# A two-layer hybrid transformer block: the odd layer's entry reordered and its second output projection begun inside the last attention block

## The chip, the cores and the metric

The kernel runs on one core of a Trainium2 chip. The metric is the device time of one execution in microseconds; a version's time is the median of its runs. The profile is that of a single execution, taken by the hardware profiler. The engines are TensorE (PE, with its weight loads as PEld), VectorE (DVE), ScalarE (ACT), GpSimd (POOL) and SyncE (SP), which issues most of the DMAs.

## What is computed

The reference runs two layers on 512 rows of x and, in the first, on 256 rows of context (ctx), all of width 1024, in float32. Layer 0 mixes with a gated MLP and a differential attention, layer 1 with a sliding-window attention with sinks. Each layer ends with a gated FFN. The change lies in layer 1's mixer and in the seam before it:

```python
a = modulate(h, norm1_g[l], sh1, sc1)            # rmsnorm(h)*(1+scale)+shift
ac = modulate(hc, norm1_g[l], csh1, csc1)
q, k, v = split(a @ w_qkv)                       # 16 heads of 64 for q, 4 for k and v
q, k = rope(q), rope(k)
kc, vc = split(ac @ w_qkv[:, 1024:])             # ctx gives keys and values only
# per block of 128 queries: scores on a band of 384 keys and on the 256 of ctx, and a sink
p = softmax([q @ k_band + mask, q @ kc, sink])
y = (p @ [v_band, vc]) @ w_out
h = h + g1 * y
h = h + g2 * swiglu(modulate(h, norm2_g[l], sh2, sc2))
```

## The kernel before, in words

Activations lie transposed: eight tiles of 128 features by 512 rows for x and by 256 for ctx. Every float32 operand of a large product is split into a rounded high part and the rest, and a product is three matmuls (`mm3`, L110, lines L114 to L116): high by high, high by rest, rest by high. A weight piece of 128 x 512 thus needs a DMA (SP), a cast (ScalarE) and a subtraction (POOL or VectorE); `unit` (L80) does this with a ring of raw buffers and slots, and `blocks` (L94) and `dense` (L104) build a full product from it. The class attribute `dve_lo` (L71) sends every n-th subtraction of `unit` to VectorE; at 0 all go to POOL.

PSUM has eight banks: four in a fixed pool (three `bank`, L52, and one `fill`, L55), and four in a second pool that is used as two `wide` of two banks each (L58) or as four `single` (L61), and is released and opened again where its use changes.

The order of instructions on each engine comes from two sources. The framework's scheduler orders them by program order as priority and by when operands and buffers come free in its own timeline. Where `run` (L46) is used, the order is written out by hand: each instruction is issued after the engine's previous one of this chain (`tail`). `issue_after` sets such an order for single instructions. The seam is chained by hand, the odd attention is not.

The seam (`seam`, L1312) goes from layer 0's FFN to layer 1's attention. It ends the FFN's last products, squares the new rows (`square`, L1346), sums them over the features by matmuls with a matrix of ones (`sums`, L1354), turns the sum of each row into a reciprocal root on the diagonal of a tile by ten small VectorE instructions (`diagonal`, L1362) and spreads it over the partitions by one more matmul (`spread`, L1381). That is the rstd of the norm. `mod` (L1427) then makes the modulated tiles: VectorE, ScalarE, and a rest on VectorE that is called later ("l"). A list of steps (L1471) interleaves for k = 0 to 7 the modulation of x ("t", "l"), the residuals of ctx ("c") and the weight loads ("w"); `products` (L1458) issues the products of x along a second list (L1455): "K" and "V" are keys and values of tile k, "s" the sums of ctx, "d" its spread. POOL adds six of ctx's squares to tile 0 after "l4", so that "s" sums two tiles. After V7 come the first of eight query projections (q0, into `fill`), ctx's keys and values for k = 0 to 7 (L1499), the rope of the keys, the stack of high and rest parts of the keys (`stack`, L1513), and copies of mask, identity and sink on VectorE (L1529).

The odd attention (`odd`, L1547) has four groups g of four heads and four query blocks i, done as two halves of two blocks. `project_q` (L1555) projects two heads, applies the rope (`rope`, L259: VectorE and POOL) and stacks (`stack_q`, L267: ScalarE and VectorE, L272 to L278). `softmax` (L1565) computes for each of four heads x the scores into a `wide` (L1584, mask L1589, ctx L1592), the maximum (L1595, L1596), the exponential (L1598) and the sums. `attend` (L1609) transposes the result through `bank` tiles (L1621), copies it (L1624), multiplies with V (L1632), and scales by the reciprocal sums, transposed at L1643, on VectorE (L1645). `keep` (L1649) splits the result for the output projection. In the first half the projections of the queries stand between the groups; the second half runs with the output projection of the first half as filler.

`project` (L1666) does the output projection of one half for m = 0 to 7 with `dense`, adds to the residual (L785) and sums squares (L798, L802). Between its two calls stand the rstd of the first half (`ffn_rstd`, L850, into `fill`), the splits of the second half, the opening of the FFN's pool (`ffn_open`, L813), and `ffn_mod` (L853), which modulates the first half of the FFN's input. The FFN (`ffn`, L869) starts with `direct` products (L973) and ends with the final norm.

## Time and profile before

| | us |
|---|---|
| median of 3 runs | 1585.23 (1578.97 to 1585.93) |
| profiled execution | 1583.56 |
| its span, first to last instruction | 1581.5 |
| mean granted TensorE clock | 0.988 |

The profiled execution is 1.67 us below the median. Three stages matter for the change:

| stage, us from the span's start | what runs |
|---|---|
| 920 to 990 | seam: ctx's rstd, K and V, first queries |
| 990 to 1184 | odd attention |
| 1184 to 1250 | second output projection, start of the FFN |

The profile's lines read "start, length, engine, line, operation, out<-in, shape"; a bracket gives the engine's idle time before the instruction and what ended it. A line L49 stands for everything that goes through `run`, so there the tile's name tells the step: `sq` for squares and sums, `sm` for the small tiles of a diagonal, `q` or `t` for a diagonal tile or a modulated one, `pw` for a tile of the second PSUM pool, `pb` for a bank, `pf` for the fill bank. In a table of stages each row has the stage, its length, the busy time and the count of instructions of PE, PEld, DVE, ACT and POOL, the granted clock as a share of full speed, the DMA share and GB/s.

### The profile page before, as it was taken

How to read it: one execution, taken by the hardware profiler on the slowest of the kernel's cores; microseconds unless marked ns; L12 is line 12 of the kernel's file. 1: busy time of each engine (PE TensorE's matmuls, PEld its weight loads, DVE VectorE, ACT ScalarE, POOL GpSimd, SP SyncE). 2: the span in 40 equal slices, each digit the busy share in tenths (PEclk: the TensorE clock that was granted, in tenths of full speed). 3: DMA queues.
4: the chain of work that ended last, by engine and by line, in shares of the span. 5: the costliest groups of instructions: out<-in, count | busy, mean ns of one | idle time of the engine just before them, and what ended most of it. 6: DMA issues, size and time to landing. Idle time of an engine off the chain costs nothing.

```text
span 1581.5 us, 24959 instructions
## 1 busy us (share of the span) xinstructions
PE 1520.5 (96%) x9547; PEld 1355.7 (86%) x9547; DVE 1082.6 (68%) x1942; ACT 728.7 (46%) x1486; POOL 831.6 (53%) x562
## 2 busy tenths in 40 slices
PE   6999988999999999999999998999999999999998
PEld 4776877889989999999999987777869989999997
DVE  4720788765697787888786478665667976666665
ACT  2412676553553333333333345555655644444444
POOL 0463211060356776777776454531304399898982
PEclk9999999999999999999999999999999999999999
DMA  9845100033123333444552211100225233333301
GB/s 329 309 143 190 40 8 1 1 133 134 67 75 119 114 110 118 140 160 141 166 167 67 74 58 42 61 28 4 72 81 198 68 96 106 97 107 105 100 21 54
DMA packets 53415, 162.26 MB, mean 103 GB/s; under 512 B 6192, under 2 KB 8624, under 8 KB 45616
## 3 DMA queue, kind: packets, MB, share of 16 engines
q1 hardware_dynamic: 46240, 135.37, 25.6%
q10 hardware_dynamic: 7056, 25.30, 4.9%
q8 instruction: 75, 1.23, 0.3%
q14 instruction: 44, 0.36, 0.1%
HBM read 158.55 MB, written 2.10 MB: 102 GB/s over the span
## 4 chain that ended last, share of the span: by engine, by line
PE 85%; DVE 10%; ACT 3%; issue 1%; POOL 0%; DMA 0%; DVEq 0%; SPq 0%; ACTq 0%; POOLq 0%
PE pw L114 11%; PE pw L115 11%; PE pw L116 11%; PE pb L115 9%; PE pb L114 8%; PE pb L116 8%; PE pf L114 4%; PE pf L115 4%; PE pf L116 4%; PE pb L1632 2%; PE pb L1621 2%; PE pf L370 2%; PE pw L1584 1%; PE pw L1592 1%; PE pw L553 1%
## 5 line engine op out<-in xcount | busy, mean ns | idle before, releaser
L114 PE MATMUL pw<-ax,w 128*128 128x384 f32 (+2 forms) x732 | 233.9, 321 | 2.5 <-DVE q L49 1.9
L115 PE MATMUL pw<-ax,w 128*128 128x384 f32 (+2 forms) x732 | 233.8, 320 | 1.4 <-DVE ax L477 1.4
L116 PE MATMUL pw<-ax,w 128*128 128x384 f32 (+2 forms) x732 | 233.2, 319 | 0.1
L785 DVE SCALAR_TENSOR_TENSOR xT<-pb,mod,xT 128x512 f32<-128x512 f32 (+3 forms) x206 | 144.1, 706 | 128.8 <-PE pb L116 128.5
L91 POOL TENSOR_TENSOR w<-raw,w 128x512 fp32r<-128x512 f32 (+1 forms) x74 | 112.8, 1531 | 204.3 <-ACT w L88 182.0
L49 POOL TENSOR_TENSOR w<-raw,w 128x512 fp32r<-128x512 f32 x120 | 182.4, 1537 | 47.1 <-ACT w L49 47.0
L49 POOL TENSOR_TENSOR w<-t,w 128x512 fp32r<-128x512 f32 x99 | 148.1, 1499 | 56.0 <-ACT w L49 56.0
L114 PE MATMUL pb<-hh,w 128*128 128x512 f32 x480 | 171.4, 357 | 2.3 <-DVE xT L785 2.3
L116 PE MATMUL pb<-hh,w 128*128 128x512 f32 x480 | 171.8, 358 | 0.3 <-DVE w L49 0.3
L115 PE MATMUL pb<-hh,w 128*128 128x512 f32 x480 | 171.5, 357 | 0.0
L115 PE MATMUL pw<-T,w 128*128 128x384 f32 (+1 forms) x508 | 157.0, 310 | 1.2 <-DVE T L131 1.2
L114 PE MATMUL pw<-T,w 128*128 128x384 f32 (+1 forms) x508 | 156.3, 310 | 1.1 <-DVE hs L49 1.1
L116 PE MATMUL pw<-T,w 128*128 128x384 f32 (+1 forms) x508 | 157.0, 310 | 0.0
L114 PEld LDWEIGHTS pw<-ax,w 128*128 128x128 f32 x732 | 139.0, 190 | 9.5 <-DVE q L49 2.6
L115 PEld LDWEIGHTS pw<-ax,w 128*128 128x128 f32 x732 | 139.3, 190 | 7.7 <-DVE ax L477 3.1
L116 PEld LDWEIGHTS pw<-ax,w 128*128 128x128 f32 x732 | 139.5, 191 | 3.0 <-DVE w L954 0.4
L114 PE MATMUL pf<-ax,w 128*128 128x256 f32 (+2 forms) x412 | 136.9, 332 | 3.9 <-ACT f L596 2.8
L115 PE MATMUL pf<-ax,w 128*128 128x256 f32 (+2 forms) x412 | 136.1, 330 | 0.8 <-POOL ax L131 0.8
L116 PE MATMUL pf<-ax,w 128*128 128x256 f32 (+2 forms) x412 | 135.6, 329 | 0.0
L49 POOL TENSOR_TENSOR hh<-hs,hh 128x768 fp32r<-128x768 f32 (+1 forms) x42 | 80.8, 1925 | 90.0 <-ACT hh L49 67.6
L49 POOL TENSOR_TENSOR w<-rawo,w 128x512 fp32r<-128x512 f32 x59 | 104.1, 1764 | 29.8 <-ACT w L49 29.8
L239 DVE SCALAR_TENSOR_TENSOR junk<-ar,cb 128x1024 bf16<-128x1024 f32 x64 | 105.7, 1652 | 0.0
(403 smaller groups left out, 3961.4 us busy)
## 6 DMA issues: line engine op xcount, KB each, us to landing
raw<-ffn_in SPq DMA_DIRECT2D x44, 1024.0 KB, 5.2
ar<-ada SPq DMA_DIRECT2D x24, 1024.0 KB, 7.2
ar<-ada ACTq DMA_DIRECT2D x48, 512.0 KB, 3.5
rawo<-ffn_out SPq DMA_DIRECT2D x88, 256.0 KB, 3.0
raw<-odd_out SPq DMA_DIRECT2D x32, 256.0 KB, 2.7
raw<-qk SPq DMA_DIRECT2D x16, 256.0 KB, 7.6
raw<-uv SPq DMA_DIRECT2D x16, 256.0 KB, 2.7
raw<-even_out SPq DMA_DIRECT2D x8, 512.0 KB, 3.5
```

Source lines behind the costliest of these rows:

```text
L49: self.tail[key] = fn(*args, **kw)
L91: eng.tensor_tensor(lo, raw, hi.bitcast(F32), ALU.subtract)
L114: mm(out, s[0], m[0], start=start, stop=False, **kw)
L115: mm(out, s[0], m[1], start=False, stop=False, **kw)
L116: return mm(out, s[1], m[0], start=False, stop=stop, **kw)
L239: return self.nc.vector.scalar_tensor_tensor(junk, t, 1.0, self.cb[who], ALU.mult, ALU.mult, accum_out=self.acc[who][:, col:col + 1])
L370: nc.tensor.matmul(ps[32 * q:32 * q + 32, :w], cst[:, k, :], t[:, w * q:w * q + w], start=k == 0, stop=k == KT - 1, skip_group_check=True)
L553: nc.tensor.matmul(ps[:, :TX], Q[c][:, qs], K[c][p][:, :TX], start=p == 0, stop=p == 1)
L785: ins = self.nc.vector.scalar_tensor_tensor(h, ps[:, r], self.modcol(l, j, m, who), h, ALU.mult, ALU.add)
L1584: nc.tensor.matmul(ps[:, st:en], Q, K[g][p][:, b0 * P:b1 * P], start=p == 0, stop=p == 1, skip_group_check=True)
L1621: last = nc.tensor.transpose(pt[:, x * P:(x + 1) * P], es[2 * (x % 2) + x // 2][:, kb * P:(kb + 1) * P], self.ident)
L1632: nc.tensor.matmul(po[64 * h:64 * h + 64, :], V[vb][:, 64 * g:64 * g + 64], t[:, h * TC:h * TC + TC], start=kb == 0, stop=kb == nb - 1, sk ...
```

## The change

In the seam, the sums of ctx move in front of K5 and take six squares directly ("s" over tiles 0, 3 to 7); only tiles 1 and 2 are added to tile 0 beforehand, one by VectorE and one by POOL. The squares of x get fewer buffers. The weights of two query projections (q0, q1) are loaded, and both projections follow V7, ahead of ctx's keys and values; q1 goes into a `single`. Mask, identity, sink and its exponential are made by ScalarE earlier, and the rope of the keys is issued before the query projections. In `odd`, the rope and stack of q0 and q1 are issued at the priority of the point after the first keys' stack, before the second PSUM pool is opened as `wide`; their stacks lie in another pool. At the end, all of the first six splits of the second half are made by VectorE, outputs m = 0 and 1 of the second projection begin with k = 0 to 5 in the fill bank, ordered after the second and the third score of the last block (g 3, i 3) and one after the other, with four weight slots taken in an order by halves of k. The spread of the first half's rstd moves behind that and into a `wide`, `ffn_mod` comes after the seventh split, and `project` finishes m = 0 and 1 with k = 6 and 7 before it goes on with m = 2.

```diff
...
-    def stack_q(self, q, pool, T, tag, bufs, s=1.0, eng=None):
+    def stack_q(self, q, pool, T, tag, bufs, s=1.0, eng=None, out=None):
         nc = self.nc
-        qa = pool.tile([P, T], F32R, name=self.uid("qa"), tag=tag, bufs=bufs)
-        qb = pool.tile([P, T], F32R, name=self.uid("qb"), tag=tag, bufs=bufs)
+        qa, qb = out or [pool.tile([P, T], F32R, name=self.uid(v), tag=tag, bufs=bufs) for v in ("qa", "qb")]
         A, B = slice(0, 64), slice(64, 128)
...
             T = (TX, TC)[who]
-            sq[who, m] = Qp.tile([P, T], F32, name=self.uid("sq"), tag=f"sq{who}", bufs=8)
+            tag, n = ("sqc", 8) if who else ("sqx", 3) if m in (0, 3, 7) else ("sqt", 2)
+            sq[who, m] = Qp.tile([P, T], F32, name=self.uid("sq"), tag=tag, bufs=n)
             run("ACT", nc.scalar.activation, sq[who, m], self.h(who, m), AF.Square)
...
             c_residual(m)
+        add("DVE", 1, 0, 1)
         c_unit(2, self.bank)
...
-        order = iter("K0 V0 K1 V1 K2 V2 K3 V3 K4 V4 K5 V5 K6 s K7 V6 d V7".split())
+        order = iter("K0 V0 K1 V1 K2 V2 K3 V3 K4 V4 s K5 V5 K6 V6 K7 d V7".split())
         csum = []
...
                     csum.append(self.single())
-                    sums(csum[0], [sq[1, 0], sq[1, 7]], TC)
+                    sums(csum[0], [sq[1, m] for m in (0, 3, 4, 5, 6, 7)], TC)
                 elif v == "d":
...
-        rests = {}
+        rests, Wq = {}, []
         for v in "t0 c5 l0 w t1 c6 t2 l1 w c3 t3 l2 w c4 t4 l3 w c7 t5 l4 t6 l5 t7 l6 l7".split():
...
                 rests.pop(k)()
-                products(f"V{k}" if k < 5 else "V5" if k == 5 else "s" if k == 6 else "K7")
-            if v == "l4":
-                for m in range(1, 7):
-                    add("POOL", 1, 0, m)
-            elif v == "l5":
+                products(f"V{k}" if k < 7 else "K7")
+            if v == "l1":
+                add("POOL", 1, 0, 2)
+            elif v in ("l5", "l7"):
                 wide, (self.ring, self.ring_cfg) = (self.ring, self.ring_cfg), kept
-                Wq = [part(*load(a["q1"][0][:, c:c + 512])) for c in (0, 512)]
+                Wq.append([part(*load(a["q1"][len(Wq)][:, c:c + 512])) for c in (0, 512)])
                 self.ring, self.ring_cfg = wide
...
         products("V7")
-        qps = self.fill()
-        for k in range(KT):
-            t, c = Wq[k // 4], k % 4 * P
-            run("PE", self.mm3, qps, (t[:, 0, c:c + P], t[:, 1, c:c + P]), X[k], k == 0, k == KT - 1)
+        mask = Rk.tile([P, 2, P], F32R, name="mask")
+        identr = Rk.tile([P, P], F32R, name="identr")
+        sink = Rk.tile([P, 16], F32, name="sink2")
+        run("ACT", nc.scalar.copy, mask, mraw.rearrange("p (a c) -> p a c", a=3)[:, 0::2, :])
+        run("ACT", nc.scalar.copy, identr, self.ident)
+        run("ACT", nc.scalar.copy, sink, nsink)
+        run("ACT", nc.scalar.mul, nsink, nsink, -1.0)
+        run("ACT", nc.scalar.activation, self.small(16), nsink, AF.Exp)
+        kfs = [Rt.tile([P, TA], F32, name=self.uid("kf"), tag="kf", bufs=2) for _ in range(2)]
+        for n in range(2):
+            self.rope(kps[n], kfs[n][:, :TX], tabs)
+        qps = [self.fill(), self.single()]
+        for ps, W2 in zip(qps, Wq):
+            for k in range(KT):
+                t, c = W2[k // 4], k % 4 * P
+                run("PE", self.mm3, ps, (t[:, 0, c:c + P], t[:, 1, c:c + P]), X[k], k == 0, k == KT - 1)
         kc = self.single()
...
                 v_c(k - 1)
-        kfs = [Rt.tile([P, TA], F32, name=self.uid("kf"), tag="kf", bufs=2) for _ in range(2)]
         K = []
-        for n in range(2):
-            self.rope(kps[n], kfs[n][:, :TX], tabs)
         for n in range(2):
...
             stack(n, slice(0, TX))
-        for n in range(2):
             nc.scalar.copy(kfs[n][:, TX:], kc[n])
             stack(n, slice(TX, TA))
-        mask = Rk.tile([P, 2, P], F32R, name="mask")
-        identr = Rk.tile([P, P], F32R, name="identr")
-        sink = Rk.tile([P, 16], F32, name="sink2")
-        with tc.issue_after(self.tail["DVE"].ins):
-            nc.vector.tensor_copy(mask, mraw.rearrange("p (a c) -> p a c", a=3)[:, 0::2, :])
-            nc.vector.tensor_copy(identr, self.ident)
-            nc.vector.tensor_copy(sink, nsink)
-            nc.vector.tensor_scalar(nsink, nsink, -1.0, None, ALU.mult)
-        with tc.issue_after(self.tail["ACT"].ins):
-            nc.scalar.activation(self.small(16), nsink, AF.Exp)
+            if n == 0:
+                here = tc.cur_priority
         V = []
...
         Rt.release()
+        self.here = here
         self.kv = qps, X, Rk, tabs, K[0] + K[1], V, mask, identr, sink, nsink
...
         tc, nc, a = self.tc, self.nc, self.a
-        self.wp.release()
-        self.open_wide()
         qps, X, Rk, tabs, K, V, mask, identr, sink, nsink = self.kv
         Rs = tc.alloc_tile_pool(name="att1", bufs=1, side="right", reuse_waits="tile")
-        Qs = {}
+        Qs, scored = {}, {}
+        stacks = [Rk.tile([P, TX], F32R, name=self.uid(t), tag="sq01", bufs=4) for _ in range(2) for t in ("qa", "qb")]
         def project_q(n):
-            ps = (self.bank if n == 1 else self.fill)() if n else qps
-            if n:
+            ps = self.fill() if n > 1 else qps[n]
+            if n > 1:
                 with tc.issue_after(self.tail["ACT"].ins) if n < 3 else ExitStack():
...
                 self.dense(ps, W, X)
-            qf = Rs.tile([P, TX], F32, name=self.uid("qf"), tag="qf", bufs=2)
+            qf = Rs.tile([P, TX], F32, name=self.uid("qf"), tag="qf", bufs=2) if n > 1 else self.tmp()
             self.rope(ps, qf, tabs)
-            Qs[n] = self.stack_q(qf, Rs, TX, "sq", 16, 0.125)
+            Qs[n] = self.stack_q(qf, Rs, TX, "sq", 12, 0.125, out=stacks[2 * n:2 * n + 2])
...
                 for p in range(2):
-                    nc.tensor.matmul(ps[:, en:en + TC], Q, K[g][p][:, TX:], start=p == 0 and not edge, stop=p == 1,
-                                     skip_group_check=True)
+                    last = nc.tensor.matmul(ps[:, en:en + TC], Q, K[g][p][:, TX:], start=p == 0 and not edge,
+                                            stop=p == 1, skip_group_check=True)
+                scored[g, i, x] = last
                 c = nm[:, x:x + 1]
...
-        raw = {}
+        raw, self.kept = {}, {}
...
             t = t[:, :TC], t[:, TC:TX]
-            self.split(*t, raw[half, n // 2][:, n % 2, :], eng)
+            self.kept[n] = self.split(*t, raw[half, n // 2][:, n % 2, :], eng)
             return t
...
         cat = []
+        with tc.high_priority(offset=tc.cur_priority - self.here):
+            for n in range(2):
+                project_q(n)
+        self.wp.release()
+        self.open_wide()
         for g in range(4):
-            project_q(2 * g)
-            project_q(2 * g + 1)
+            if g:
+                project_q(2 * g)
+                project_q(2 * g + 1)
             attend(g, 0)
...
-        def project(half, cat, bank):
-            for m in range(KT):
+        def project(half, cat, bank, ready=()):
+            for m, ps, W in ready:
+                for k in (6, 7):
+                    self.mm3(ps, W[k], cat[k], False, k == 7)
+                self.residual(1, 2, m, half * TC, TC, ps)
+                self.square(sq, m, half * TC, TC, rest[half], (8, 7)[half])
+            for m in range(len(ready), KT):
                 ps = bank(m)[:, :TC]
...
         project(0, cat, lambda m: self.fill())
-        self.ffn_rstd(sq, rest[0], TX // 2)
-        catB = [keep(1, n, nc.gpsimd if n % 2 else nc.vector) for n in range(8)]
+        dg = self.rstd_diag([(sq[:, :TC], TC)], 1.0 / D, self.fill, None, None, rest[0])[0]
+        catB = [keep(1, n, nc.vector) for n in range(6)]
+        both, ready, mark = self.fill(), [], None
+        slots = [self.slot() for _ in range(4)]
+        for m in range(2):
+            W = []
+            for u in range(2):
+                hi, lo = self.unit(a["odd_out"][m, :, u * 512:u * 512 + 512], 512, slots[2 * u + m])
+                W += [(hi[:, c:c + P], lo[:, c:c + P]) for c in range(0, 512, P)]
+            ps = both[:, m * TC:(m + 1) * TC]
+            with tc.issue_after(scored[3, 3, 1 + m].ins):
+                for k in range(6):
+                    with tc.issue_after(mark.ins) if mark else ExitStack():
+                        ins = self.mm3(ps, W[k], catB[k], m == k == 0, False)
+            mark = ins
+            ready.append((m, ps, W))
+        self.dve_lo = 1
+        catB += [keep(1, n, nc.gpsimd if n % 2 else nc.vector) for n in range(6, 8)]
+        self.r = self.spread(dg, self.wide)
         Rs.release()
...
         self.ffn_open(1)
-        self.ffn_mod(1, 0)
-        self.dve_lo = 1
-        project(1, catB, lambda m: self.bank())
+        with tc.issue_after(self.kept[6].ins):
+            self.ffn_mod(1, 0)
+        project(1, catB, lambda m: self.bank(), ready)
         self.sq = sq, rest[1]
...
```

## Prediction

> **What bounds the kernel now.** I read the page first, its engine line and its chain of work that ended last.
>
> ```profile
> PE 1520.5 (96%) x9547; PEld 1355.7 (86%) x9547; DVE 1082.6 (68%) x1942; ACT 728.7 (46%) x1486; POOL 831.6 (53%) x562
> ...
> PE 85%; DVE 10%; ACT 3%; issue 1%; POOL 0%; DMA 0%; DVEq 0%; SPq 0%; ACTq 0%; POOLq 0%
> ```
>
> TensorE is busy for 96% of the span and carries 85% of the chain. So a change gains only where TensorE stands idle or runs at a lower clock, or where it is given less work. The change touches about 900 to 1270 us. The waits of TensorE in that stretch, longest in total first, name the places:
>
> ```profile
> PE pw L49 <- DVE q L49: 4.8, 1, 4.8
> PE pb L1621 <- ACT e L1598: 3.1, 6, 1.5
> PE pw L1584 <- DVE qa L278: 1.8, 1, 1.8
> PE pb L116 <- DVE w L91: 1.6, 1, 1.6
> ...
> PE pf L194 <- DVE sa L1600: 1.1, 1, 1.1
> ...
> PE pb L1632 <- ACT pt L1624: 0.6, 1, 0.6
> ```
>
> I then looked each one up in the timeline of TensorE (start, length, instruction, in brackets the idle time before it) and read the granted clock around it from the stage table (PEclk is the third column from the end; 0.50 is half speed).
>
> ```profile
> 956.36 1.22 PE L49 MATMUL pw<-q,ones 128*128 128x256 f32 x2 [4.77 <-DVE q L49]
> 954.00:956.00 2.00, 0.00 (x0) 0.00 (x0) 1.86 (x5) 1.72 (x3) 1.43 (x2) 0.54 0.00 0
> 956.00:961.00 5.00, 4.64 (x17) 4.27 (x18) 4.88 (x9) 3.98 (x8) 0.00 (x0) 0.50 0.00 0
> 990.83 0.38 PE L1584 MATMUL pw<-kh,qa 128*128 128x256 f32 x1 [1.76 <-DVE qa L278]
> 992.00:995.00 3.00, 3.00 (x8) 2.30 (x7) 2.86 (x5) 0.05 (x1) 2.84 (x2) 0.50 0.35 99
> 1160.03 0.67 PE L194 MATMUL pf<-q,ones 128*128 128x256 f32 x2 [1.09 <-DVE sa L1600]
> 1178.09 0.44 PE L1621 MATMUL pb<-ident,e 128*128 128x128 f32 x2 [1.48 <-ACT e L1598]
> 1179.14 0.89 PE L1632 MATMUL pb<-pt,v 128*64 128x256 f32 x4 [0.62 <-ACT pt L1624]
> 1179.00:1183.00 4.00, 3.86 (x16) 1.93 (x16) 0.34 (x2) 0.68 (x2) 0.61 (x1) 0.57 0.94 395
> 1195.44 0.39 PE L116 MATMUL pb<-ax,w 128*128 128x256 f32 x1 [1.60 <-DVE w L91]
> 1196.00:1200.00 4.00, 4.00 (x23) 4.00 (x22) 4.00 (x4) 3.10 (x7) 4.00 (x4) 0.57 0.24 72
> ```
>
> There are four stalls: the rstd of ctx (4.77 us), the first query of the odd attention (1.76), the last attention block (1.48 + 0.62), and a weight of the second output projection (1.60). After each, TensorE works some microseconds at half clock, and half of that time is lost as well. After the first, from 956.36 to 961 it is 4.64 us, so 2.3 us lost. In the others the mean clock gives it: (1 - 0.57) x 4 = 1.7 us in each of the last two, and at least (1 - 0.50) x 3 = 1.5 us after the first query.
>
> **Part 1: ctx's sums earlier.** Today the sums stand on TensorE between K6 and K7, and only K7 and V6 lie between them and the matmul that spreads the rstd ("d").
>
> ```profile
> 943.52 0.40 PE L114 MATMUL pw<-ax,w 128*128 128x512 f32 x1
> 946.34 0.40 PE L114 MATMUL pw<-ax,w 128*128 128x512 f32 x1
> 947.73 1.05 PE L49 MATMUL pw<-ones,sq 128*128 128x128 f32 x8
> 941.30 2.42 DVE L49 SCALAR_TENSOR_TENSOR ax<-t,mod,ax 128x512 fp32r<-128x512 f32 x2
> 948.81 0.16 DVE L49 TENSOR_SCALAR sm<-pw 128x2 f32<-128x2 f32 x1 [5.09 <-PE pw L49]
> 920.50 2.84 PE L49 MATMUL pf<-ones,sq 128*128 128x128 f32 x24
> 923.38 0.16 DVE L49 TENSOR_SCALAR sm<-pf 128x4 f32<-128x4 f32 x1 [1.97 <-PE pf L49]
> 925.15 0.69 DVE L49 SCALAR_TENSOR_TENSOR q<-sm,ident 128x512 f32<-128x512 f32 x1
> ```
>
> K5 starts at 943.52 and K6 at 946.34, so one K and V pair is 2.82 us. VectorE has done the last x tile at 941.30 + 2.42 = 943.7 and then waits 5.09 us for the sums. With the sums after V4 they start at 943.5. Six tiles are summed in place of two, 24 rows in place of 8. The x sums are the same 24 rows: 2.84 us against 1.05, so **+1.8 us** of TensorE work. They end near 946.3. The diagonal is ten small VectorE instructions, for x from 923.38 to 925.84, 2.5 us; for ctx today it takes 948.81 to 956.3, 7.5 us, because the rope of K and POOL's work lie in it. Now K5, V5, K6, V6 and K7 cover it: 2 x 2.82 + 1.4 = 7.0 us. So even the slow 7.5 us would be late by only about half a microsecond, and VectorE has nothing else to do until K7 ends. I take the stall as gone: -4.8 and -2.3 of half clock, +1.8. **Sum -5.3 us**; with the slow diagonal it is -4.8 plus perhaps the half clock, -2.5 as the weak end. The two adds that remain (VectorE one, POOL one) lie under x's work and cost nothing; five POOL adds go, and the two weight casts of the second query that POOL now does earlier take their place.
>
> **Part 2: two query projections ahead, stacks ready.** The order on TensorE changes from q0, ctx's K and V, q1, q2, scores to q0, q1, ctx's K and V, q2, scores.
>
> ```profile
> 959.93 0.63 PE L114 MATMUL pf<-ax,w 128*128 128x512 f32 x1
> 965.88 0.28 PE L114 MATMUL pw<-ax,w 128*128 128x256 f32 x1
> 977.39 0.40 PE L114 MATMUL pb<-ax,w 128*128 128x512 f32 x1
> 988.10 0.40 PE L116 MATMUL pf<-ax,w 128*128 128x512 f32 x1
> ```
>
> ctx's 96 matmuls run from 965.88 to 977.39, 11.5 us or 0.12 each; q1 and q2 take 977.39 to 988.33, 5.5 each. Moving q1 adds no work. What it buys is time: rope and stack of q0 and q1 are four POOL, eight VectorE and four ScalarE instructions that now lie under the 11.5 us of ctx's products. Today q1's product ends 5.5 us after 977.39, its rope and stack come after that, and the scores wait 1.76 for a stacked query. That wait and its half clock go, **-1.8 - 1.5 = -3.3 us**, if VectorE keeps up. Its work there:
>
> ```profile
> L1519 DVE TENSOR_TENSOR kl<-kf,kh 64x512 fp32r<-64x512 f32 x8 | 5.5, 685 | 0.1
> L49 DVE SCALAR_TENSOR_TENSOR ax<-t,mod,ax 128x256 fp32r<-128x256 f32 x8 | 4.3, 543 | 0.2 <-ACT ax L49 0.2
> L49 DVE SCALAR_TENSOR_TENSOR t<-ctxT,mod,pw 128x256 f32<-128x256 f32 x8 | 3.8, 480 | 0.2
> ...
> L1531 DVE CAST identr<-ident 128x128 fp32r<-128x128 f32 x1 | 1.3, 1328 | 0.0
> ```
>
> K's stack 5.5, ctx's modulation 4.3 + 3.8, the rope of K, two query ropes and stacks and the ctx part of K's stack: I estimate 9 us for the last three from wide VectorE rows near 0.7 us each. That is 23 us from the end of K7 (953.3) to 976, and q2 keeps TensorE busy until about 983. Mask, identity and sink move to ScalarE, which idles there, and free VectorE of 1.3 us for the identity alone. The weights of q1 are two more DMAs on SP and two casts each on ScalarE and POOL; SP has nothing else, and q2's weights wait for q0's slots, free since about 961. If the cover fails, the scores wait for VectorE: from 0 up to the 3.3 us gained, and I take 0, with 2 as likely under contention.
>
> **Part 3: the second output projection inside the last block.** Outputs 0 and 1 get their products for k = 0 to 5, 36 matmuls x 0.12 = 4.3 us, released by the scores of the last block and held in the one fill bank. The holes there are 1.48 + 0.62 = 2.1 us, so half of the 4.3 fills holes (-2.1) and the half clock after them goes (-1.7). The spread of the first half's rstd leaves the block, which frees the 1.09 of L194 (-1.1). The rest is only moved. The four weight units that this needs are loaded and cast as today; POOL subtracts them in place of VectorE.
> The other side is what follows the block:
>
> ```profile
> 1184.86 0.37 PE L114 MATMUL pb<-ax,w 128*128 128x256 f32 x1
> 1183.72 0.86 DVE L863 SCALAR_TENSOR_TENSOR hm<-xT,mod,pf 128x256 f32<-128x256 f32 x2
> 1186.85 0.68 DVE L1645 TENSOR_TENSOR o<-o,pb 128x512 f32<-128x512 f32 x1
> 1188.20 0.33 SPq L85 DMA_DIRECT2D raw<-odd_out  x1
> ```
>
> Today TensorE has 48 matmuls (5.8 us) with weights at hand at 1184.86, and still waits at 1195.44 for a weight whose DMA was issued at 1188.20. Now 12 of them are left, 1.4 us. In return the two slots that hold k = 0 to 3 come free inside the block, so output 2's weights can be ready (24 matmuls, 2.9 us). ffn_mod now waits for kept[6], behind the product at L1645, where it started at 1183.72 before; its result, on which the first FFN products rest, comes about 3 us later against the block's end unless the shorter queue gives it back. So the wait for weights may go (-1.6 - 1.7) or grow by 4.3 us. I take +2, between the ends. **Sum -2.1 - 1.7 - 1.1 + 2 = -2.9 us.**
>
> **Sum.** -5.3 - 3.3 - 2.9 = -11.5 us.
>
> ```profile
> 1200.00:1250.00 50.00, 50.00 (x418) 49.92 (x417) 40.65 (x93) 25.45 (x60) 12.62 (x7) 1.00 0.39 137
> ```
>
> From 1200 to 1250 TensorE has no idle time, so what is gained ahead of it is carried on. The profiled execution took 1583.56 (span 1581.5), so 1572.1; the median of the three runs is 1585.23, which gives 1573.7. I predict **1573**, between the two.
>
> [...] After the 4.77 us of idle time the clock fell, but also after 1.76 (0.50 at 992 to 995). [...]
>
> **The rivals.**
> 1. *The clock stays.* The half clock at 992 and 1179 has another cause than the short holes. Then 1.5 + 1.7 us of the sum are not gained: -8.3, 1576. [...] 0.10.
> 2. *VectorE becomes the bound* before the first scores and after the block. Only part 1 and a bit more remain: -3 to -7, 1578 to 1582. For it: VectorE was busy 4.88 of 5 us at 956 to 961 and its instructions stretch when POOL works; against it: the free 5 us before the sums. 0.24.
> 3. *Slower: starvation after the last block.* Place: the four-slot weight ring and ffn_mod behind kept[6]. TensorE has only 12 matmuls at hand. If output 2's weights too come only behind ffn_mod on VectorE, TensorE idles from 1.4 us after the block until ffn_mod and then a DMA, a cast and a subtraction are through. Today the next weight comes 1195.44 - 1184.86 = 10.6 us after the block; with ffn_mod 3 us later, 13.6. That is 12.2 us idle in place of 1.6, and two half clock windows in place of one (+1.7): +12.3, less 4.9 inside the block. With parts 1 and 2 at their weak ends (-2.5 and -1) the result is 4 us slower, about 1589. It decides from 8.4 us of added idle time on. For it: VectorE was 4.00 of 4 us busy at 1196 to 1200. 0.09.
> 4. *It does not do what it says:* the scheduler, which orders the attention itself, puts the moved matmuls behind the block and reorders the rest; within 3 us of before. 0.08.
> 5. *All works* and the wait for weights goes too: -15 to -18, 1567 to 1570. 0.09.
> The forecast, -8 to -15, has 0.40.
>
> About 0.5% (8 us) is what a measurement of this kernel can tell from no change. Faster by more: nearly all of the forecast and rival 5, half of rival 1, a little of 2, 0.56. Within: the rest of these, most of 2, 4 and some of 3, 0.36. Slower: 0.08. The range leaves out the far end of rival 5 and most of rival 3: 1565 to 1586.
>
> **What would show it.** Right: no wait of the ctx spread for q at L49 and a clock of 1.00 around it; the sums as 24 rows ahead of K5; first scores near 983 with no wait for qa; matmuls of the output projection among the last block's transposes, and no clock of 0.50 there. Wrong: a long wait for a weight (L91) or for an ax tile after the block, a wait for kl or qa at L1584, or more idle time spread over the attention between 1000 and 1170, where today's order is lucky and the new one need not be.

## The result, and the profile after

The changed kernel takes **1576.85 us** (median; 1574.92 to 1580.41), the kernel before 1585.43 beside it: ratio 0.9958, 95% interval 0.9945 to 0.9970. That is 4.8 to 8.7 us faster, 6.7 in the middle, where -11.5 was forecast. The two medians lie 8.6 us apart, at the upper end of that interval; in the later measurements the kernel before has medians of 1582.80 to 1583.22.

The profiled execution after took 1580.41 us, 3.6 above its median, and its seam begins 3.1 us later than in the profile of before (x sums at 923.58 against 920.50), though nothing ahead of it was changed. So below, stages are counted from the x sums of each profile, or by their own length.

The engine line and the chain, of the kernel after:

```profile
PE 1517.3 (96%) x9563; PEld 1356.5 (86%) x9563; DVE 1078.7 (68%) x1938; ACT 727.8 (46%) x1490; POOL 826.8 (52%) x558
...
PE 85%; DVE 10%; ACT 3%; issue 1%; DMA 0%; POOL 0%; DVEq 0%; SPq 0%; ACTq 0%; POOLq 0%
```

They look as before: 3.2 us of TensorE's time are gone and the share of the chain is the same. The waits of TensorE from 900 to 1270 say more (line, total, times, longest):

```profile
PE pw L1584 <- ACT e L1599: 3.2, 1, 3.2
PE pb L1622 <- ACT e L1599: 2.5, 4, 1.5
PE pw L115 <- DVE ax L49: 2.2, 1, 2.2
...
PE pw L114 <- ACT T L130: 1.5, 1, 1.5
PE pf L114 <- DVE qf L263: 1.4, 1, 1.4
PE pw L114 <- DVE hh L862: 1.1, 1, 1.1
PE pw L115 <- DVE T L131: 1.1, 1, 1.1
PE pb L1633 <- ACT pt L1625: 0.6, 1, 0.6
...
PE pb L116 <- DVE w L91: 0.4, 1, 0.4
```

Of the waits that the prediction named, four are gone or nearly so: 4.8 for the diagonal of ctx, 1.8 for the first query, 1.1 for L194, 1.6 for a weight. In their place stand waits that were not there: 3.2 for an exponential between the first scores, 2.2 for a modulated tile of ctx, 1.1 for an FFN tile (hh) 5 us behind the last block, and 1.5 + 1.1 for T, the modulated tiles behind the second spread. Waits of 1.5 for an exponential and of 0.6 still stand, the first of them at another place (see part 3 below).

The places themselves, from TensorE's timeline:

```profile
946.54 2.84 PE L49 MATMUL pw<-ones,sq 128*128 128x128 f32 x24
956.24 0.60 PE L49 MATMUL pw<-q,ones 128*128 128x256 f32 x2
978.67 0.39 PE L115 MATMUL pw<-ax,w 128*128 128x256 f32 x1 [2.19 <-DVE ax L49]
992.98 0.39 PE L1584 MATMUL pw<-kh,qb 128*128 128x256 f32 x1 [3.20 <-ACT e L1599]
1176.97 0.29 PE L114 MATMUL pf<-ax,w 128*128 128x256 f32 x1
1177.33 0.59 PE L194 MATMUL pw<-q,ones 128*128 128x256 f32 x2
```

ctx's sums start at 946.54, as 24 rows in 2.84 us, and its spread follows at 956.24 without a wait; projection matmuls stand inside the last block, up to 1176.97, and the spread at 1177.33 has no wait. So the instructions stand where the change puts them. The clock around these places (window, length, TensorE's busy time, granted clock, DMA share, GB/s):

```profile
955.00:960.00 5.00, 5.00 (x30) 1.00 0.00 0
...
990.00:1000.00 10.00, 7.02 (x36) 1.00 0.19 55
...
1170.00:1185.00 15.00, 14.18 (x106) 1.00 0.49 190
1200.00:1250.00 50.00, 47.37 (x366) 0.93 0.34 122
```

The clock is full at the spread of ctx and in the last block, where it was 0.50 and 0.57. But from 1200 to 1250, where TensorE had no idle time at all before, it now idles for 2.6 us at a mean clock of 0.93. This is the stretch on which the sum relied.

### The profile page after: what moved, and what is told of

It is laid out like the page before. It is cut to its first block, busy times and chain, and to the rows that moved or that the text cites. A ratio compares the mean times of both kernels' runs of the same rounds, so it can differ in the third digit from the quotient of the medians.

```text
span 1578.6 us, 24990 instructions
## 1 busy us (share of the span) xinstructions
PE 1517.3 (96%) x9563; PEld 1356.5 (86%) x9563; DVE 1078.7 (68%) x1938; ACT 727.8 (46%) x1490; POOL 826.8 (52%) x558
## 4 chain that ended last, share of the span: by engine, by line
PE 85%; DVE 10%; ACT 3%; issue 1%; DMA 0%; POOL 0%; DVEq 0%; SPq 0%; ACTq 0%; POOLq 0%
PE pw L114 12%; PE pw L115 12%; PE pw L116 11%; PE pb L115 8%; PE pb L116 8%; PE pb L114 8%; PE pf L114 4%; PE pf L115 4%; PE pf L116 4%; PE pb L1633 2%; PE pb L1622 2%; PE pf L369 2%; PE pw L1584 1%; PE pw L1592 1%; DVE t L49 1%
## 5 line engine op out<-in xcount | busy, mean ns | idle before, releaser
L115 PE MATMUL pw<-ax,w 128*128 128x384 f32 (+2 forms) x740 | 236.6, 320 | 4.2 <-DVE ax L49 2.2
L114 PE MATMUL pw<-ax,w 128*128 128x384 f32 (+2 forms) x740 | 235.8, 322 | 3.6 <-DVE q L49 1.9
L116 PE MATMUL pw<-ax,w 128*128 128x384 f32 (+2 forms) x740 | 236.1, 320 | 0.1
L91 POOL TENSOR_TENSOR w<-raw,w 128x512 fp32r<-128x512 f32 (+1 forms) x76 | 114.9, 1521 | 218.2 <-ACT w L88 195.6
L49 POOL TENSOR_TENSOR w<-raw,w 128x512 fp32r<-128x512 f32 x122 | 185.9, 1539 | 48.5 <-ACT w L49 48.3
L114 PE MATMUL pf<-ax,w 128*128 128x256 f32 (+2 forms) x428 | 141.5, 331 | 4.2 <-ACT f L595 2.8
L115 PE MATMUL pf<-ax,w 128*128 128x256 f32 (+2 forms) x428 | 140.3, 328 | 0.0
L116 PE MATMUL pf<-ax,w 128*128 128x256 f32 (+2 forms) x428 | 140.1, 327 | 0.0
```

The costliest lines, as they stand in the source:

```text
L49: self.tail[key] = fn(*args, **kw)
L91: eng.tensor_tensor(lo, raw, hi.bitcast(F32), ALU.subtract)
L114: mm(out, s[0], m[0], start=start, stop=False, **kw)
L115: mm(out, s[0], m[1], start=False, stop=False, **kw)
L116: return mm(out, s[1], m[0], start=False, stop=stop, **kw)
```

## The experiments

All ratios are to the kernel before on the same chip. The two columns on the right are from the profiles: how much earlier (-) than in the profile of before the last attention block ends and the first residual after the FFN's output products comes, both counted from the x sums.

| kernel | ratio, 95% interval | end of block, us | FFN residual, us |
|---|---|---|---|
| the change | 0.9958 (0.9945 to 0.9970) | -5.0 | -5.0 |
| e1 part 1 alone | 1.0002 (0.9992 to 1.0012) | -1.5 | -1.5 |
| e2 parts 1 and 2 | 0.9957 (0.9942 to 0.9971) | -5.8 | -6.8 |
| e3 part 3 alone | 1.0014 (1.0004 to 1.0025) | +1.6 | +2.7 |
| e4 parts 1 and 3 | 1.0006 (0.9997 to 1.0014) | +1.8 | +0.4 |
| e5 part 1, masks on ScalarE | 1.0003 (0.9990 to 1.0015) | -0.5 | -0.5 |
| e6 part 1, two banks | 1.0241 (1.0222 to 1.0260) | +38.0 | +36.7 |
| e7 the change, half of L91 on GpSimd | 0.9952 (0.9934 to 0.9970) | -5.2 | -6.7 |
| e8 parts 1 and 2, q2's weights early | 0.9963 (0.9948 to 0.9978) | -6.5 | -6.5 |
| e9 part 1, queries' low parts on GpSimd | 0.9967 (0.9954 to 0.9981) | -6.3 | -6.3 |
| e10 part 2 alone | 0.9965 (0.9951 to 0.9978) | -4.0 | -4.1 |
| e11 the change, all of L91 on GpSimd | 0.9973 (0.9962 to 0.9983) | -3.8 | -4.3 |
| e12 parts 1 and 2, low parts on GpSimd | 0.9956 (0.9941 to 0.9970) | -5.0 | -6.2 |

### The parts one by one: e1 to e4

Part 1 is the order of ctx's sums and the adds that belong to it, part 2 the seam's second query projection, the stacks and the masks, part 3 everything in `project` and around it. The core of part 1:

```diff
-        order = iter("K0 V0 K1 V1 K2 V2 K3 V3 K4 V4 K5 V5 K6 s K7 V6 d V7".split())
+        order = iter("K0 V0 K1 V1 K2 V2 K3 V3 K4 V4 s K5 V5 K6 V6 K7 d V7".split())
...
-                    sums(csum[0], [sq[1, 0], sq[1, 7]], TC)
+                    sums(csum[0], [sq[1, m] for m in (0, 3, 4, 5, 6, 7)], TC)
```

e1, part 1 alone:

> The kernel before with the sums of ctx moved ahead of K5 and nothing else of the change (one query projection in the seam, everything after it as before). Theory A (each part pays what its holes on TensorE were worth; part 2 then gives most of part 1 back because VectorE and the late weights of q2 and q3 become the bound): 5 us faster than before, ratio 0.997, the wait of the ctx spread for q at L49 gone and no half clock near it; the wait for a stacked query at L1584 stays. Rival B (the sums only move the wait: q0 and the ctx products then wait for the modulation of ctx): 0 to 2 us faster.

e2 leaves out part 3, so `project` and what stands around it are those of before:

> The changed kernel with the end of the odd layer as before: parts 1 and 2, without the second output projection inside the last block. Theory A: less than the sums alone, about 3 us faster than before (ratio 0.998), with the wait for an ax tile of ctx (2 us) and the wait at L1584 (3 us) of the changed kernel. Rival B (part 2 pays as I forecast and those waits are particular to one execution): 8 us faster, ratio 0.995.

e3 is the kernel before with part 3 alone; e4 adds part 1 to that:

> The kernel before with part 3 alone: the second output projection begun inside the last block, spread and ffn_mod moved, seam and first queries as before. Theory A: 5 to 6 us gained at the end of the output projection, of which about 2 are lost again between 1225 and 1260 where VectorE's sums for the FFN are the bound: 3 to 4 us faster, ratio 0.9975. Rival C (the end region gains nothing in the whole, all comes from the seam): 0 to 1 us.

> Parts 1 and 3 without part 2: sums early and the end as changed, but q1 after the products of ctx as before. Theory A (the parts add, part 2 costs): 8 to 9 us faster than before, ratio 0.9945, and so 2 us faster than the whole change. Rival B (part 2 pays): slower than the whole change by 3 us, about 5 faster than before.

Measured: nothing for part 1 alone, the whole gain for parts 1 and 2, a small loss for part 3 alone (0.6 to 4 us), nothing for parts 1 and 3. My first theory, that the parts add up, falls: part 1 did exactly its work at its place in all of them (the first query projection starts 4.9 us earlier in e1, e2, e4 and the change; -5.3 was forecast), and yet in e1 3.4 us of it are gone before the block ends.

Where they go is seen in the stages from the start of the first query projection to the first scores, on to the end of the last query projection, and on to the end of the last block. Before, then the first two in e1 (the columns are those of the clock table above):

```profile
959.93:988.33 28.40, 28.40 (x169) 0.98 0.18 56
988.33:1039.17 50.84, 48.03 (x257) 0.97 0.19 58
1039.17:1185.10 145.93, 139.88 (x1027) 0.99 0.14 46
```

```profile
955.59:987.30 31.71, 28.68 (x171) 1.00 0.13 43
987.30:1039.76 52.46, 46.25 (x257) 1.00 0.19 61
```

Before, TensorE had no idle time ahead of the first scores, which fits a VectorE that used the hole at ctx's sums to get ahead. In e1 it idles 3.0 us there and 6.2 us in the second stage, where before it idled 2.8. So 6.4 us of idle time come back, more than the 4.8 that went; that only 3.4 show in this pair of profiles is the clock, which is 1.00 in all three stages of e1 and below it in those of before. The waits of e1, TensorE's from 900 to 1270 and VectorE's from 985 to 1015, name the tile:

```profile
PE pf L114 <- DVE qf L263: 6.9, 4, 2.9
```

```profile
DVE qa L278 <- ACT qa L272: 9.7, 5, 2.7
```

A query projection goes into the one fill bank, and the next may start only when the rope on VectorE (L262, L263) has read it. The timeline of e1's VectorE shows what stands ahead of a rope whose projection ended at about 1004.2 (last matmul 1003.85):

```profile
1004.36 1.35 DVE L278 SCALAR_TENSOR_TENSOR qa<-qf,qa 64x512 fp32r<-64x512 f32 x1 [2.61 <-ACT qa L272]
1005.74 1.78 DVE L278 SCALAR_TENSOR_TENSOR qb<-qf,qb 64x512 fp32r<-64x512 f32 x1
...
1007.45 0.71 DVE L262 STREAM_SHUFFLE sh<-pf 128x512 f32<-128x512 f32 x1
```

The low parts of the query before (qa, qb) stand ahead of it, and they wait 2.61 us for ScalarE's high part. ScalarE was held up itself, by what stood ahead in its queue:

```profile
1001.84 0.69 ACT L1599 ACTIVATE e<-pw,sa 128x512 f32<-128x512 f32 x1 [4.56 <-DVE sa L1597]
...
1003.69 0.64 ACT L272 ACTIVATE qa<-qf 64x512 fp32r<-64x512 f32 x1
```

GpSimd ended its half of that query's rope at 1001.72, but two exponentials, which had waited for VectorE's maxima (sa), and the cast of a weight came before the high part. TensorE's next projection starts at 1008.94, 2.87 us late. So there is a loop: TensorE into the one bank, the rope on VectorE and GpSimd, the high part on ScalarE, the low part on VectorE, then the next rope, one turn per query. The loop was there before the change: in before, VectorE's wait for qa is 2.61 us at the same place, at 1004.84, 84.3 us after the x sums. In e1 it is 83.3 us after them, so of 4.9 us only one is left there. What is new is that TensorE comes early and waits: 6.9 us for qf, 1.0 before. Two theories remained: that VectorE simply has too much to do before the first scores (A), or that the one bank and the order behind it set the pace (B).

### Load or order: e5, e6, e9

e5 is e1 with four small operations taken from VectorE, as part 2 does it:

```diff
-            nc.vector.tensor_copy(mask, mraw.rearrange("p (a c) -> p a c", a=3)[:, 0::2, :])
-            nc.vector.tensor_copy(identr, self.ident)
...
+        run("ACT", nc.scalar.copy, mask, mraw.rearrange("p (a c) -> p a c", a=3)[:, 0::2, :])
+        run("ACT", nc.scalar.copy, identr, self.ident)
```

> ctx's sums moved alone, and beside them only the masks, the identity, the sink and its exponential given to ScalarE; the second query projection stays where it was. Theory A: the 4.9 us that the sums gain are lost to VectorE, which is full before the first scores (4.1 us of it on these small operations); without them the waits of the query projections for qf (L263, 6.9 us in the run with the sums alone) fall by about half and the block ends 2 to 4 us earlier than in before: ratio 0.9975 to 0.999. Rival B: the one fill bank sets the pace of the query projections, whatever VectorE has to do: the waits for qf stay, ratio 1.000 plus or minus 0.001.

e6 is e1 with a second bank for the queries:

```diff
-            ps = (self.bank if n == 1 else self.fill)() if n else qps
+            ps = (self.bank if n % 2 else self.fill)() if n else qps
```

> ctx's sums moved alone, and beside them the odd query projections written to the rotating banks, so that two projections don't wait for one bank; VectorE has all its work. Rival B: the waits for qf (6.9 us in the run with the sums alone) go, and the block ends 3 to 5 us earlier than in before: ratio 0.997 to 0.998. Theory A: the next projection's rope and stack are behind the same VectorE work, so the wait goes to the scores instead: ratio 0.999 to 1.001.

e5 gives nothing: the waits for qf stay at 6.2 us, so theory A falls. In e1's second stage, too, VectorE is busy for 36.74 of 52.46 us and waits 11.3 us for qa: it lacked no time, it stood waiting. e6 missed both expectations, by far: 2.4% slower. Its stages from the first scores to the last query projection in the fill bank, and on to the end of the last block, and one of its waits (total, times, longest) with its worst case:

```profile
988.42:1036.30 47.88, 39.86 (x206) 0.89 0.12 39
1036.30:1224.84 188.54, 162.59 (x1077) 0.90 0.13 43
```

```profile
PE pw L1585 <- DVE qa L278: 12.2, 2, 7.3
```

```profile
1073.82 0.58 PE L1585 MATMUL pw<-kh,qa 128*128 128x256 f32 x1 [7.27 <-DVE qa L278]
```

The projections in the fill bank are done 4.6 us earlier, but those in the rotating banks now come late. The last two start only at 1060.63 and 1098.14, where in e1 the last of all ends at 1039.8, and the scores of their group wait right behind them, 7.3 and 5.0 us, for their stacks. TensorE idles 26 us in the last stage and runs at 0.90. So e6 changed the order of the projections with the bank, and it doesn't answer what the one bank costs; why the scheduler puts them so late was not looked into.

e9 goes at the order instead. It is e1 with the low parts of the queries' stacks, from the third query on, on GpSimd. The factor 0.125 goes to the keys' stacks, so that the low part of a query is a plain subtraction, as GpSimd does it for the weights:

```diff
-            Qs[n] = self.stack_q(qf, Rs, TX, "sq", 16, 0.125)
+            Qs[n] = self.stack_q(qf, Rs, TX, "sq", 16, 1.0, nc.vector if n < 2 else nc.gpsimd)
...
-                nc.scalar.copy(kh[X, c], k)
+                nc.scalar.mul(kh[X, c], k, 0.125)
```

> ctx's sums moved alone, and beside them the low parts of the queries' stacks (L278, from the third query on) made by GpSimd instead of VectorE; so that GpSimd can do them, the factor 0.125 goes from the queries to the keys' stacks, which is exact. Theory E: with the sums alone the 4.9 us are lost because VectorE, in order, stands before qa (9.7 us in 5 waits for ScalarE's L272) while the next projection's rope, which frees the one bank, is behind it (rope L262 at 1007.45, 3.3 us after its projection's end). Without qa in VectorE's queue the waits of TensorE for qf (6.9 us) fall to 4 or less and the block ends 3 to 5 us earlier than in before: ratio 0.996 to 0.998. Rival F: GpSimd, with the rope's second half and the low parts, takes the place of VectorE in the chain, or the scores wait for qa: ratio 0.999 to 1.004.

Theory E is borne out. The wait for qf falls from 6.9 to 2.7 us, and the second stage from 52.46 to 44.80. Of these 7.7 us 4.3 are idle time; the rest is work, 19 matmuls, that now comes in the third stage:

```profile
PE pf L114 <- DVE qf L263: 2.7, 3, 1.7
```

```profile
956.30:988.03 31.73, 28.67 (x170) 1.00 0.13 43
988.03:1032.83 44.80, 42.84 (x238) 1.00 0.22 71
```

With part 1 alone and the loop loosened the ratio is 0.9967, or 3.0 to 7.3 us: the 4.9 us now arrive. The profile, in which the clock is 1.00 in all of these stages as in e1's, has the block's end 4.8 us earlier than e1's. The first stage is the same 31.7 us in both, so what e1 lost in it stays lost. GpSimd is now busy for 42.83 of the 44.80 us of the second stage, so there is little room for more of this.

### Part 2 without part 1: e10, and two attempts at more: e8, e12

e10 is part 2 alone; "s" stands after K6 as before, with POOL's six adds.

> The second part of the change alone: the second query projection ahead of ctx's products, its rope and both stacks ahead, the masks on ScalarE; ctx's sums stay after K6 as in before (the buffers of the squares are those of the changed kernel, for the room). Theory E: the second part breaks the chain of ropes before the first scores, but the sums' 4.8 us hole in TensorE stays: the block ends 1 to 4 us earlier, ratio 0.9975 to 0.9995, and the two parts together (0.9957) are more than the sum of each alone. Rival G: the second part alone is the whole gain and the sums nothing: ratio 0.995 to 0.9965.

```profile
PE pw L49 <- DVE q L49: 5.6, 1, 5.6
...
PE pf L114 <- DVE qf L263: 1.1, 1, 1.1
```

The hole at ctx's sums is there in full (5.6 us), the waits for qf are 1.1, as before the change (1.0), and the ratio is 0.9965: the edge of G's range, while the block's end, -4.0, is the edge of E's. Part 2 alone is worth 3.5 to 7.8 us. The profile doesn't account for all of it: of the 4.0 us at the block's end 1.3 are idle time, the wait for qa (1.8) gone and one for an exponential (1.4) in its place among others, and 2.7 are a fuller clock in that one execution. Part 1 on top of it (e2) adds 1.3 us by the middles, which the intervals don't tell from nothing; in the profiles the block ends 1.8 us earlier with it. So part 1 is worth nothing alone and little beside part 2. What part 2 does for it is seen in TensorE's wait for qf: 6.9 us with part 1 alone, 1.1 in e2.

e8 is e2 without the order that puts the third query's weights behind ScalarE's last work of the seam; e12 is e2 with e9's low parts on GpSimd:

```diff
-                with tc.issue_after(self.tail["ACT"].ins) if n < 3 else ExitStack():
-                    W = self.blocks(a["q1"][n])
+                W = self.blocks(a["q1"][n])
```

> The first two parts of the change without the third (0.9957 measured), and the third query projection's weights no longer ordered behind ScalarE's last work of the seam. If their lateness (the casts at 980 and 985, the first with 3.4 us of waiting for the DMA) costs the holes of 2.2 and 3.2 us before the first scores, the block ends 1 to 3 us earlier than in that run: ratio 0.994 to 0.995. Rival: ScalarE's casts come between the mixing steps that TensorE needs, and the gain is nothing or a loss of up to 2 us: ratio 0.9955 to 0.997.

> The first two parts of the change, without the third, and the low parts of the queries' stacks on GpSimd as in the run with the sums alone (where that took 5 us off the run with the sums alone). If what is left of VectorE's waits for ScalarE's halves (4.0 us in 2) still costs TensorE its 2.8 us of idle time while the queries are projected, the block ends 1 to 3 us earlier than with the two parts (0.9957): ratio 0.994 to 0.995. Rival: the second part already took those waits out of the chain, both are cures of one loss: ratio 0.995 to 0.997, and with GpSimd's 1.3 us a piece not lower.

Neither gains on e2: 0.9963 and 0.9956 against 0.9957. The rivals are borne out. In particular part 2 and e9 look like two cures of what part 1 loses in the loop: each brings the gain, and both together (e12) bring no more than part 2 does. It fits that with the first two queries ahead of the loop it turns less often while the scores wait; no run shows that apart.

### The end: e7 and e11

e3 shows part 3 by itself, against the kernel before. Three stages: from the end of the last query projection to the end of the last block, on to the second spread (L194), and on to the first residual of the FFN. Before (its first row, 145.93 us, is shown above), then e3:

```profile
1185.10:1227.02 41.92, 40.28 (x317) 0.96 0.57 200
1227.02:1258.45 31.43, 30.07 (x235) 1.00 0.07 20
```

```profile
1040.07:1187.75 147.68, 142.72 (x1062) 1.00 0.14 45
1187.75:1227.88 40.13, 38.64 (x307) 0.96 0.59 213
1227.88:1262.15 34.27, 30.24 (x209) 0.90 0.06 17
```

Up to the end of the block 36 matmuls more, 4.3 us of work, cost 1.75 us. The idle time falls by 1.1 us (6.05 to 4.96); the rest is the clock, 0.99 to 1.00. The places of e3, with the last block's transposes first:

```profile
1179.77 0.27 PE L1622 MATMUL pb<-ident,e 128*128 128x128 f32 x1
1161.49 0.44 PE L1622 MATMUL pb<-ident,e 128*128 128x128 f32 x2 [1.48 <-ACT e L1599]
1183.32 0.65 PE L1633 MATMUL pb<-pt,v 128*64 128x256 f32 x4 [0.62 <-ACT pt L1625]
```

In the last block the hole of 1.48 us is filled: projection matmuls stand between its scores and transposes from 1173.65 on, and no transpose there waits for an exponential. The 0.62 stay. The gain of L194 did not come. Where the spread of before stood (1160.03, behind 1.09 us of waiting), the transposes that follow it now wait for an exponential themselves, 1.48 us at 1161.49, which the spread and its wait had covered. So 1.48 are filled and 0.39 are lost, which is the 1.1.

Behind the block, 36 matmuls fewer are due before the spread, yet the count falls by 10 only. The traces of the change and of e2 say why: 26 products of the FFN's first half (into `pw`), which stood behind the spread, now stand ahead of it, 141 in place of 115. The stage gains 1.8 us in place of 4.3. The 26 products (3.1 us) that covered the chain of spread, mixing and T behind the spread are spent. TensorE now waits in this chain, 1.5 and 1.1 us for T in e3 as in the change, and runs at a clock of 0.90: with 26 products less, this stage takes 2.8 us more. Idle time is 2.7 of it; the half clock costs about the 3.1 us that the missing products would have saved, and this share differs between executions (e4 and e7, at 0.95, take 32.0 and 31.3 us for the stage). In the change, a stretch of half clock follows those waits:

```profile
1223.00:1228.00 5.00, 2.37 (x13) 0.90 0.00 0
1228.00:1234.00 6.00, 6.00 (x30) 0.51 0.01 3
```

Why did the scheduler put filler there instead of the projection? Theory C was that the projection's weights pace it: they all go over VectorE. The change's SyncE waits, where before the same line has 24.9 us:

```profile
SPq L85 <- DVE w L91: 47.1, 8, 20.2
```

Between its L91 at 1193.52 and the next at 1201.19 VectorE works for the FFN's first half (L131 among it), a residual and the sums of squares. e7 sends half of L91 to GpSimd, and e11 (with 0) all of it:

```diff
-        self.dve_lo = 1
+        self.dve_lo = 2
```

> The changed kernel with one number changed: of the low parts of the second output projection's weights (L91) every second one is made by GpSimd instead of all by VectorE. Theory C: behind the last block the second projection is paced by its weights: SyncE waits 47 us in 8 times for L91 on VectorE before it may load the next piece, the last residual comes at the same time with 36 matmuls fewer, and the filler of the FFN's first half is used up. Freed, the second spread (L194) comes 1 to 3 us earlier and the waits for T and hh behind it shrink: 1572 to 1575, ratio 0.992 to 0.9945. Rival D: the rows' chain from the last block through the residuals bounds it, or GpSimd's slower subtraction (about 2 us for 128x512) delays the weights as much: within 1 us of the changed kernel.

> The changed kernel with all low parts of the second projection's weights (L91) on GpSimd, none on VectorE. Half of them on GpSimd didn't bring the second spread forward (-6.6 us against -6.8, counted from the x sums). Theory C, last chance: VectorE's queue still held the other half behind the FFN's first mixing; with none there the spread comes at least 1 us earlier than in the changed kernel: ratio 0.992 to 0.9945. Rival D: weights aren't what paces it, or GpSimd's 1.3 to 1.7 us for each of 12 is as slow: spread the same or up to 3 us later, ratio 0.995 to 0.998.

The spread did not come earlier: by the profiles -6.6 (e7) and -4.8 (e11), against -6.8 in the change. Theory C falls in this form, the more so as in e11 TensorE waits for no weight of L91 at all and still 1.6 and 1.6 us for T. e7's time (0.9952) is not to be told from the change's. GpSimd is no free place, as e7's rows for L91 on the two engines show (min/median/max in ns):

```profile
L91 POOL TENSOR_TENSOR w<-raw,w x5: 1287/1298/1741, 1182.4 to 1206.5; 128x512 fp32r<-128x512 f32 x5
...
L91 DVE TENSOR_TENSOR w<-raw,w x5: 693/1359/1782, 1187.7 to 1207.0; 128x512 fp32r<-128x512 f32 x5
```

What the traces show is that the gain ends in filler moved ahead of the spread and in waits in the chain behind it. That the one causes the other is read from them; whether holding back those 26 products, or the FFN's preparation on both engines, would return the gain was not tried and stays open.

## Why the prediction was right and wrong

The measured 1576.85 lies in the range and 4 us above the forecast. The band given for the forecast, -8 to -15, is missed by the middle of the measurement: -6.7 is in that of the second rival, -3 to -7, and the interval reaches into both. That the sum landed in the range is luck in part: measured by themselves, its terms of -5.3, -3.3 and -2.9 are +0.3, -5.5 and +2.2 by the middles (e1, e10, e3).

- **Part 1, -5.3:** right in size at its place (-4.9 at the first query projection, no wait, full clock), wrong in what it is worth: nothing alone (e1). The step that failed is the silent one, that a matmul that starts earlier ends the stage earlier: 4.8 us of idle time went and 6.4 came back behind it. VectorE was judged by its load; what counted was an order, qa ahead of the next rope, with ScalarE in the loop (e5, e9).
- **Part 2, -3.3:** the wait named for it (1.76 for qa) went, but one of 3.2 for an exponential, which the sum had at nothing, stands between the first scores of the change (1.4 in e10). Alone the part is -5.5 by the middle of e10, and how much of that is the wait and how much the clock is not shown. Beside part 1 it does what the sum had no term for: TensorE's wait for qf, 6.9 us in e1, is 1.4 in the change. The text had the right cover (ropes and stacks under ctx's products), and only half of the reason.
- **Part 3, -2.9:** measured between nothing (the change against e2) and 2 us of loss (e3). Of the 2.1 us of holes 1.48 were filled; the 1.1 of L194 did not come and turned into a loss of 0.4, since a wait for an exponential lay hidden behind the spread's. The clock in the block rose by 1.5 us of time, near the 1.7 priced. The term that was mis-sized most is the +2 for what follows, which measured +5.3 in e3: of the 4.3 us taken from the second projection the next stage gives back 1.8 (2.5 lost), and the FFN's start costs 2.8. Rival 3's starvation for weights did not come; that wait fell from 1.6 to 0.4.
- **"What is gained ahead of it is carried on":** it held for parts 1 and 2 (e2: -5.8 at the block's end, -6.8 at the FFN's residual). It failed for part 3. A full TensorE from 1200 to 1250 hid a chain over the spread, VectorE and ScalarE: with 3.1 us less of cover in e3 it shows 2.6 us of waits for T, so by these figures it was about half a microsecond shorter than its cover.
- **Rival 1, the clock:** the sum doesn't decide it, but the half clocks were priced too surely; see the last section.
- **Rival 2, VectorE becomes the bound:** right in place and size, not in kind. Before the first scores VectorE was not out of time (e5: its four small operations elsewhere, no gain); it stood still in its queue.

## What to carry to other kernels

When a stall is removed, look for the next loop between engines that the stall had given time to, and read the in-order queues, not the busy shares: in e1 the rope that TensorE needed stood behind a `qa` that waited 2.61 us, and TensorE waited 2.87. Ask of every matmul that is moved ahead which hole it was filling, because filler that is spent early can leave a latency chain uncovered later (part 3: waits of 1.5 and 1.1 us for T). When a wait is taken away, look for a second one that lies behind it (in e3 the 1.48 us for the exponential behind L194's spread). And run the parts alone and in pairs: here one part was worth nothing alone, one nothing at all, and the sum of the three terms landed in the range for reasons other than those given.

## What the runs showed of the hardware

In these profiles the length of a short hole does not decide the clock. Before, 0.50 followed a hole of 1.76 us. After the change, holes of 2.19 and 3.20 us were followed by a full clock (the first in the row below, the second from 990 to 1000), and two of 1.5 and 1.1 by a half one (0.51 from 1228 to 1234). What does decide it was not shown. I had put every half clock down to the hole ahead of it and priced its removal: that is not a price that one profile can give. The same stretch of program shows it. From the first query projection to the first scores TensorE's order is the same in the change, e2, e7 and e11, with the same hole of 2.2 us in it; the change and e11 take 29.6 us at a clock of 1.00, and e2 and e7 31.1 at 0.95. The change, then e2, the last line with the wait that follows in e2 (3.20 in the change, at 992.98 above):

```profile
958.10:987.75 29.65, 27.46 (x167) 1.00 0.09 27
```

```profile
959.14:990.27 31.13, 28.96 (x167) 0.95 0.10 32
```

```profile
994.01 0.38 PE L1584 MATMUL pw<-kh,qb 128*128 128x256 f32 x1 [1.71 <-ACT e L1598]
```

And the 1.5 us of half clock were not lost: the exponential behind them came at its own time. The score that waits for it starts 34.9 us after the first query projection in the change and in e2 alike, with 1.5 us less of waiting in e2. Half clock ahead of a wait for another engine can cost nothing.

The same subtraction of 128 x 512 on VectorE (L91) takes 0.69 to 1.78 us in e7 (rows above), and 0.68 to 1.79 us in the profile of before. There the three at 1193.72, 1197.01 and 1200.39 take 1.67 to 1.79 us, with GpSimd at work from 1193.56 to 1203.33; the eight from 1203.54 to 1213.90 take 0.68 or 0.69 us, with GpSimd idle. Counting such instructions at 0.7 us each, as the prediction did for VectorE's load, can miss by up to a factor of 2.6 in just the stretches in which both engines work.
